# One tile more for split weights, one raw slot less, and expert weights through all slots in one turn

## Chip, core and metric

The kernel runs on one core of a Trainium2 chip. The metric is the device time of one execution in microseconds (us), and smaller is better. Engines: TensorE (PE in the rows; PEld is its weight load), VectorE (DVE), ScalarE (ACT), GpSimd (POOL) and SyncE (SP), whose queue issues nearly all transfers from device memory.

## What is computed

256 tokens of width 2048 in float32 go through a first block of two layers and a second block of one layer with experts. Cut to what matters:

```python
def first_block(x, ...):
    for l in range(2):
        proj = rms_norm(x, norm_g[l]) @ w_in[l]          # 2048 x 6726
        # three attentions on slices of proj: decay heads, latent heads (w_uq, w_ukv),
        # and differential heads; each gated with silu
        x = x + concat([a_out, b_out, c_out]) @ w_out[l]  # 2048 x 2048
    return rms_norm(x, final_norm_g)

def second_block(x, c, ...):
    mod = silu(c) @ w_ada + b_ada                         # six rows of 2048
    proj = modulate(rms_norm(x, g_mix), ...) @ w_in       # two banded attentions
    x = x + gt1 * (concat([norm(o_a), norm(o_b)]) @ w_out)
    h = modulate(rms_norm(x, g_ffn), ...)
    for e in range(32):                                   # top 1 group, top 2 experts in it
        a = silu(h @ w_gate[e]) * (h @ w_up[e])           # 2048 x 512 each
        y = y + combine[:, e:e+1] * (a @ w_down[e])       # 512 x 2048
    x = x + gt2 * y
    modf = silu(c) @ w_ada_final + b_ada_final
    return modulate(rms_norm(x, g_final), ...)
```

## The kernel before

**Projections.** Weights stream through on-chip memory once. `wload` (line 131) takes a "raw" slot (`rawt`, line 116; four slots of 1 MB, 8 KB on each of 128 partitions) and issues a load of up to four blocks of 128 rows by 512 columns on SP's queue. `proj` (line 301) goes over the four raw tiles of a projection; each raw tile is split in two halves. `wsplit` (line 269) takes an "hl" tile, also 1 MB (three slots), and `split` (lines 265 to 267) fills it from half a raw tile: ScalarE casts the weights to the high part (L266) and VectorE subtracts it from them for the low part (L267). `mm` then does three matmul passes (high by high, high by low, low by high), with the weights as the stationary operand (L291) or the moving one (L295): 24 matmuls of 256 columns or 12 of 512 for an hl tile of 512 columns. `uq` and `qsplit` split in their own order of columns, into hl tiles too.

**Modulation on the side.** After each hl tile `tick` advances a generator (`ada_gen`, line 546) at a rate of 0.59: it loads a 0.5 MB piece of `w_ada` into one of three "araw" slots on SP's queue (L543) and lets VectorE multiply it by a column of silu(c) and add it (L561), two pieces ahead.

**Experts.** Each of the 32 experts has eight 1 MB tiles for gate and up (`load_gu`, line 1174) and four for down (`load_d`, line 1193). The slots are those of the projections and no others: `etile` (line 1154) hands out the next of a list of tags, here nine (five "xm" of the seven slots of the transposed activations, one hl, the "ada" accumulator, two hl) to gate and up tiles; down tiles take the four raw slots. The first expert's loads begin while the last output projection runs (line 1204), three of them in slots of another tag ("p", `ewp` in the rows). Four experts are gathered at a time (`quad`); after the first four, two xm tiles are taken for the accumulator y. Down weights of the last expert come as strips (`load_d_strip`, line 1201).

**Order.** The lists of the engines are not written out by hand. The tile framework walks the program, gives out slots when they come free in its own estimate of time, and so fixes the order on each engine and queue; on the chip each queue keeps that order. A load into a slot waits on its queue for the slot's last user.

Of the kernel before, what the change touches and what calls it, by code (L numbers as in the profile page):

```python
# [10 lines left out]
F32 = mybir.dt.float32  # L11
F32R = mybir.dt.float32r
# [8 lines left out]
P = 128  # L21
D = 2048
# [72 lines left out]
def tile_kernel(tc, a, out, dbg=None):  # L95
# [8 lines left out]
    big = es.enter_context(tc.tile_pool(name="big", bufs=1))  # L104
# [9 lines left out]
            nc.sync.dma_start(dbg[name], ap)  # L114

    def rawt(shape, name):
        return big.tile(shape, F32, tag="raw", bufs=4, name=name)

    def pslot(shape, dt, name):
        return big.tile(shape, dt, tag="p", bufs=7, name=name)  # L120

    def small(n, name):
        return sm.tile([P, n], F32, tag=f"s{n}", name=name)
# [3 lines left out]
    def uid(s):  # L127
        cnt[0] += 1
        return f"{s}{cnt[0]}"

    def wload(w, k0, nk, n0, n, name):
        t = rawt([P, nk, n], name)
        nc.sync.dma_start(t, w[k0 * P : (k0 + nk) * P, n0 : n0 + n].rearrange("(k p) n -> p k n", p=P))
        return t
# [130 lines left out]
    def split(dst_hi, dst_lo, src):  # L265
        A.copy(dst_hi, src)  # L266
        V.tensor_sub(dst_lo, src, dst_hi)  # L267

    def wsplit(view, name, n):
        t = big.tile([P, 2, 2, 512], F32R, tag="hl", bufs=3, name=name)  # L270
        split(t[:, 0, :, :n], t[:, 1, :, :n], view)
        return t

# [2 lines left out]
    def tb_ops(n, bank=0):  # L276

        return [("T", P * i, P, bank + i // 2, 256 * (i % 2)) for i in range(n)]

    def nb_ops(c, m):  # L280

        return [("N", c, m, tb, 0, tb) for tb in range(2)]

    def mm(acc, started, w, xk, ops, last):
        for op in ops:
            kind, c, m, b, o = op[:5]
            for j, (u, v) in enumerate(PASS):
                st = b not in started
                started.add(b)
                if kind == "T":  # L290
                    T.matmul(acc[:m, b, o : o + 256], w[:, u, c : c + m], xk[v], start=st, stop=last and j == 2,  # L291
                             skip_group_check=True)
                else:
                    tb = op[5]
                    T.matmul(acc[:, b, o : o + m], xk[v][:, P * tb : P * tb + P], w[:, u, c : c + m], start=st,  # L295
                             stop=last and j == 2, skip_group_check=True)

    def accum(name=None):
        return pa.tile([P, 2, 512], F32, tag="acc", name=name or uid("acc"))

    def proj(w, n0, n, xT, ops, qs=(0, 1, 2, 3), acc=None, started=None, final=True, k0=0, splitter=None, pre=None, mid=None, by_op=False):

        acc = accum() if acc is None else acc
        started = set() if started is None else started
        for q in qs:
            raw = wload(w, k0 + 4 * q, 4, n0, n, uid("raw"))
            raws = [raw[:, 2 * hf : 2 * hf + 2, :] for hf in range(2)]
            if pre:
                pre(q)
            end = final and q == qs[-1]  # L310
            hls = []
            for hf in range(2):
                hl = (splitter or wsplit)(raws[hf], uid("hl"), n)
                hls.append(hl)
                if end and by_op:
                    continue
                for kk in range(2):
                    mm(acc, started, hl[:, :, kk, :], [xT[q][:, v, 2 * hf + kk, :] for v in range(2)], ops,
                       end and hf == 1 and kk == 1)
                if mid and hf == 0:  # L320
                    mid(q)
                tick()
            if end and by_op:
                for op in ops:
                    for k in range(4):
                        mm(acc, started, hls[k // 2][:, :, k % 2, :], [xT[q][:, v, k, :] for v in range(2)], [op], k == 3)
        return acc
# [32 lines left out]
    def xTtile(name):  # L360
        return big.tile([P, 2, 4, S], F32R, tag="xm", bufs=7, name=name)
# [237 lines left out]
    def layer(l, xT, ssq):  # L599
# [65 lines left out]
        def rope(dst, src):  # L665
            ps = pt.tile([P, 512], F32, tag="tp", name=uid("rp"))
            T.matmul(ps[:, :S], cst["perm"], src, start=True, stop=True)
            t = wk.tile([P, S], F32, tag="m", bufs=3, name=uid("rt"))
            V.tensor_mul(t, ps[:, :S], cst["sinT"])
            V.tensor_mul(dst, src, cst["cosT"])  # L670
            V.tensor_add(dst, dst, t)
# [11 lines left out]
        def uq():  # L683
            qn = pslot([P, 6, S], F32, uid("qn"))
            for u in range(3):
                acc = accum()
                started = set()
                for hf in range(2):
                    hl = big.tile([P, 2, 2, 512], F32R, tag="hl", bufs=3, name=uid("hl"))
                    raw = wload(a["w_uq"][l], 2 * hf, 2, 384 * u, 384, uid("raw"))  # L690
                    v4 = raw.rearrange("p k (h c) -> p k h c", h=2)
                    for c0, c1, o in ((0, 128, 0), (128, 192, 256)):
                        w_ = c1 - c0
                        for kk in range(2):
                            dh = hl[:, 0, kk, o : o + 2 * w_].rearrange("p (h c) -> p h c", h=2)
                            dl = hl[:, 1, kk, o : o + 2 * w_].rearrange("p (h c) -> p h c", h=2)
                            split(dh, dl, v4[:, kk, :, c0:c1])
                    for kk in range(2):
                        mm(acc, started, hl[:, :, kk, :], [c_[:, 2 * hf + kk, :] for c_ in cqT], tb_ops(3),
                           hf == 1 and kk == 1)  # L700
                A.copy(qn[:, 2 * u : 2 * u + 2, :], acc[:, 0, :].rearrange("p (j t) -> p j t", j=2))
                qr = wk.tile([P, S], F32, tag="m", bufs=3, name=uid("qr"))
                A.copy(qr, acc[:, 1, 0:S])
                rope(ropes[:, u, :], qr)
            return qn
# [40 lines left out]
        if l == 0:  # L746
            startup_rest()
            ada_start()
        rope(ropes[:, 3, :], kr[:, 0, :])
        qn = uq()  # L750
        kn, vb = ukv()
        if l == 0:
# [4 lines left out]
        for h in range(6):  # L757
# [5 lines left out]
            t = wk.tile([P, 384], F32, tag="t", bufs=3, name=uid("t"))  # L763
# [43 lines left out]
        for h in range(6):  # L807
# [4 lines left out]
            t = wk.tile([P, 384], F32, tag="t", bufs=3, name=uid("t"))  # L812
# [15 lines left out]
        for g in range(2):  # L828
            t = pslot([P, 4, S], F32, uid("cqk"))
# [26 lines left out]
        for h in range(4):  # L856
            ts_, rs = [], []
            halves = [slice(64 * i, 64 * i + 64) for i in range(2)]
            for ps in scores_pair([[(qsl(cqh[z, h, :]), ckh[z, h, :])] for z in halves]):
                t = wk.tile([P, 384], F32, tag="t", bufs=3, name=uid("t"))  # L860
# [77 lines left out]
    with tc.high_priority():  # L938
        vs = []
        for ss in (ssq, ssq1):  # L940
            t = small(2, uid("rr_s"))
# [3 lines left out]
        t = small(2, "rr_t")  # L945
# [8 lines left out]
    for q in range(4):  # L954
        t = xTtile(uid("hT"))
# [19 lines left out]
    w_in = a["w_in_2"][0]  # L975

    def qsplit(view, name, n):
        t = big.tile([P, 2, 2, 512], F32R, tag="hl", bufs=3, name=name)
        for hf in range(2):
            src = view[:, :, 256 * hf : 256 * hf + 256].rearrange("p k (r c) -> p k r c", c=64)  # L980
            dh, dl = [t[:, v].rearrange("p k (r a c) -> p k r a c", a=2, c=64)[:, :, :, hf, :] for v in range(2)]
            split(dh, dl, src)
        return t
# [157 lines left out]
    def add_half(s, acc, r):  # L1141
        for tb in range(2):
            xs = x[:, tb, 512 * s : 512 * s + 512]
            u = wk.tile([P, 512], F32, tag="stage", bufs=3, name=uid("u"))
            V.scalar_tensor_tensor(u, acc[:, tb, :], r[:, tb : tb + 1], gt1(s), op0=OP.mult, op1=OP.mult)
            V.tensor_add(xs, xs, u)

    for s in range(4):
        add_half(s, proj(a["w_out_2"][0], 512 * s, 512, mT2b, nb_ops(0, 512), qs=(0, 1), k0=8), rb_)
    wtags = ["xm"] * 5 + ["hl", "ada", "hl", "hl"]  # L1150
    wbufs = {"raw": 4, "hl": 3, "xm": 7, "ada": 1}
    wn = [0]

    def etile(shape, tag=None):
# [5 lines left out]
    def eload(src, shape, tag=None):  # L1160
        t = etile(shape, tag)
        nc.sync.dma_start(t, src)
        return t
# [25 lines left out]
    def d_rows(e):  # L1189

        return a["w_down_2"][0, e].rearrange("(p j) n -> p j n", j=4)

    def load_d(e):
        r = {}
        for f in range(4):
            t = eload(d_rows(e)[:, f, :], [P, D], "raw")
            for s in range(4):
                r[f, s] = t[:, 512 * s : 512 * s + 512]
        return r

    def load_d_strip(e, c0, n, f, nf):
        return eload(d_rows(e)[:, f : f + nf, c0 : c0 + n], [P, nf, n], "raw")

    gu0 = load_gu(0, GU0[:6])

# [224 lines left out]

    gu0.update(load_gu(0, GU0[6:]))
    d0 = load_d(0)

    def rows(c, t):
# [53 lines left out]
    for q in range(LAST + 1):  # L1488
        i = q % 2
        for b in range(NQ):  # L1490
            e = NQ * q + b
# [33 lines left out]
    for c0, n in STRIPS:  # L1525
        m = n // 4
        nf = 2048 // n
# [59 lines left out]
```

## Time and profile before

| What | us |
|---|---|
| median of three runs (2361.89, 2363.03, 2366.7) | 2363.03 |
| the profiled execution's own time | 2382.56 |
| its span, first to last instruction | 2380.9 |
| TensorE busy (89% of the span) | 2118.8 |
| TensorE weight load busy (64%) | 1512.5 |
| VectorE busy (53%) | 1252.7 |
| ScalarE busy (33%) | 793.1 |

The mean granted clock of TensorE is 0.949 of full speed, and 760.82 MB move at a mean of 320 GB/s. The busy time of TensorE is modelled (its matmuls are pipelined), so the waits say more than the shares. Rows of waits give the engine and line that waited, what it waited for, the time in total, how often, and the longest. Rows of a timeline give start and length, engine, line, operation, output and inputs, a count, and in brackets the idle time before it with what ended it. "SPq" is an issue on SP's queue.

### The profile page before, as it was taken

How to read it: one execution, taken by the hardware profiler on the slowest of the kernel's cores; microseconds unless marked ns; L12 is line 12 of the kernel's file. 1: busy time of each engine (PE TensorE's matmuls, PEld its weight loads, DVE VectorE, ACT ScalarE, POOL GpSimd, SP SyncE). 2: the span in 40 equal slices, each digit the busy share in tenths (PEclk: the TensorE clock that was granted, in tenths of full speed). 3: DMA queues.
4: the chain of work that ended last, by engine and by line, in shares of the span. 5: the costliest groups of instructions: out<-in, count | busy, mean ns of one | idle time of the engine just before them, and what ended most of it. 6: DMA issues, size and time to landing. Idle time of an engine off the chain costs nothing. (4 is left out here: it accounts for less than half of the span.)

```text
span 2380.9 us, 32560 instructions
## 1 busy us (share of the span) xinstructions
PE 2118.8 (89%) x12919; PEld 1512.5 (64%) x12919; DVE 1252.7 (53%) x1990; ACT 793.1 (33%) x1583; POOL 99.9 (4%) x149
## 2 busy tenths in 40 slices
PE   8999999999999999899999988869677878686975
PEld 8989997789899977798786774324232424241421
DVE  5786687876776877776766871202121212121323
ACT  5453645545535545545555421101010101010111
POOL 0000100000100000202001000000000000000000
PEclk9999999999999999999999989989898989899998
DMA  6688796786787876796856889999999999999995
GB/s 216 217 300 289 229 332 242 244 297 190 249 312 248 306 272 219 226 341 187 319 195 222 297 325 376 421 421 422 421 420 421 421 421 421 421 420 421 421 421 239
DMA packets 220888, 760.82 MB, mean 320 GB/s; under 512 B 22448, under 2 KB 43260, under 8 KB 172344
## 3 DMA queue, kind: packets, MB, share of 16 engines
q1 hardware_dynamic: 215576, 750.88, 83.3%
q0 software_dynamic: 4960, 7.71, 1.4%
q8 instruction: 103, 1.69, 0.3%
q14 instruction: 57, 0.47, 0.1%
q10 hardware_dynamic: 192, 0.08, 0.0%
HBM read 755.68 MB, written 2.97 MB: 319 GB/s over the span
## 5 line engine op out<-in xcount | busy, mean ns | idle before, releaser
L266 ACT CAST hl<-raw 128x1024 fp32r<-128x1024 f32 (+4 forms) x478 | 423.8, 897 | 503.0 <-PE acc L291 252.5
L267 DVE TENSOR_TENSOR hl<-raw,hl 128x1024 fp32r<-128x1024 f32 (+4 forms) x478 | 487.7, 1033 | 145.9 <-ACT hl L266 145.0
L291 PE MATMUL acc<-xT,hl 128*128 128x256 f32 x3744 | 471.7, 286 | 8.6 <-DVE hl L267 5.6
L291 PEld LDWEIGHTS acc<-xT,hl 128*128 128x128 f32 x3744 | 458.1, 193 | 14.3 <-DVE hl L267 6.7
L561 DVE SCALAR_TENSOR_TENSOR ada<-araw,cact,ada 128x1024 f32<-128x1024 f32 x240 | 307.2, 1287 | 96.2 <-DMA araw<-in_w_ada_dram 79.9
L1393 PE MATMUL gu<-ew,xe 128*32 128x512 f32 x1528 | 237.7, 634 | 89.3 <-DMA ew<-in_w_up_dram 59.4
L1406 DVE SCALAR_TENSOR_TENSOR eth<-eth,guT 128x128 f32<-128x128 f32 x32 | 9.2, 288 | 448.6 <-ACT eth L1405 448.6
L1398 ACT COPY gus<-gu 128x512 f32<-128x512 f32 x32 | 18.8, 586 | 615.5 <-PE gu L1393 615.5
L1393 PEld LDWEIGHTS gu<-ew,xe 128*32 128x32 f32 x1528 | 51.7, 113 | 261.7 <-issue 103.4
L295 PE MATMUL acc<-hl,mT 128*128 128x512 f32 x768 | 188.4, 397 | 1.7 <-DVE hl L267 1.7
L1415 PE MATMUL acc<-ew,aT 128*32 128x512 f32 x992 | 159.1, 772 | 23.9 <-DVE aT L1408 22.2
L291 PE MATMUL acc<-hT,hl 128*128 128x256 f32 x1248 | 168.7, 289 | 2.9 <-DVE hl L267 2.9
L291 PEld LDWEIGHTS acc<-hT,hl 128*128 128x128 f32 x1248 | 156.2, 193 | 12.6 <-issue 9.2
L295 PEld LDWEIGHTS acc<-hl,mT 128*128 128x128 f32 x768 | 141.9, 189 | 34.4 <-issue 3.7
L295 PE MATMUL acc<-hl,xT 128*128 128x512 f32 (+1 forms) x768 | 158.1, 367 | 5.4 <-DVE hl L267 5.4
L295 PEld LDWEIGHTS acc<-hl,xT 128*128 128x128 f32 x768 | 132.3, 190 | 30.4 <-DVE hl L267 7.8
L1371 PEld LDWEIGHTS xg<-oh,xres 128*128 128x128 f32 x512 | 122.8, 328 | 36.8 <-issue 26.8
L1419 DVE TENSOR_TENSOR y<-acc,gt2A 32x512 f32<-32x512 f32 x93 | 63.6, 684 | 148.1 <-PE acc L1415 147.1
L1371 PE MATMUL xg<-oh,xres 128*128 128x128 f32 x512 | 131.4, 411 | 5.4 <-ACT C L1362 3.2
L1393 PE MATMUL gu<-ew,xet 128*32 128x512 f32 x504 | 93.4, 663 | 35.3 <-DMA ew<-in_w_up_dram 26.0
L295 PE MATMUL acc<-hl,oT 128*128 128x512 f32 x384 | 101.6, 413 | 0.2 <-DVE hl L267 0.2
L1415 PEld LDWEIGHTS acc<-ew,aT 128*32 128x32 f32 x992 | 32.8, 133 | 103.7 <-issue 62.6
(339 smaller groups left out, 2017.5 us busy)
## 6 DMA issues: line engine op xcount, KB each, us to landing
ew<-in_w_up_dram SPq DMA_DIRECT2D x128, 1024.0 KB, 19.8
ew<-in_w_down_dram SPq DMA_DIRECT2D x128, 1024.0 KB, 19.8
ew<-in_w_gate_dram SPq DMA_DIRECT2D x126, 1024.0 KB, 19.8
raw<-in_w_in_dram SPq DMA_DIRECT2D x124, 1024.0 KB, 7.1
araw<-in_w_ada_dram SPq DMA_DIRECT2D x192, 512.0 KB, 6.3
raw<-in_w_out_dram SPq DMA_DIRECT2D x48, 1024.0 KB, 6.4
araw<-in_w_ada_final_dram SPq DMA_DIRECT2D x64, 512.0 KB, 6.3
raw<-in_w_in_dram SPq DMA_DIRECT2D x16, 512.0 KB, 3.6
```

The costliest lines, as they stand in the source:

```text
L266: A.copy(dst_hi, src)
L267: V.tensor_sub(dst_lo, src, dst_hi)
L291: T.matmul(acc[:m, b, o : o + 256], w[:, u, c : c + m], xk[v], start=st, stop=last and j == 2, skip_group_check=True)
L295: T.matmul(acc[:, b, o : o + m], xk[v][:, P * tb : P * tb + P], w[:, u, c : c + m], start=st, stop=last and j == 2, skip_group_check=True)
L561: V.scalar_tensor_tensor(ah, raw, ck, ah, op0=OP.mult, op1=OP.add)
L1371: T.matmul(ps[:, m * j : m * j + m], quads(x[:, tb, :], k), oh[:, tb, :], start=j + tb == 0, stop=tb == 1, skip_group_check=True)
L1393: T.matmul(ps[c : c + CAP, :], xe(i, k + d)[:, CAP * b : CAP * b + CAP], gu(v, k + d), start=k == 0, stop=k == KT - 2, skip_group_check=True)
L1398: A.copy(g, ps)
L1406: V.scalar_tensor_tensor(th, th, 1.0, v4[:, :, 0:CAP], op0=OP.add, op1=OP.mult)
L1415: T.matmul(acc[CAP * s : CAP * s + CAP, 0, :], aT[:, f, :], wd(f, s), start=f == 0, stop=f == 3, skip_group_check=True)
L1419: V.tensor_mul(yv(i, s)[CAP * b : CAP * b + CAP, :], acc[h, 0, :], gt2(s)[h, :])
```

## The change

Raw slots go from four to three and hl slots from three to four, so the memory is the same. The list of tags for expert tiles gets 13 entries in place of nine, all slots of all four tags (xm five), and down tiles and the last expert's strips take the next of this list instead of a raw slot. The whole diff but for the third and fourth place where an hl tile is taken (`uq`, `qsplit`), which change in the same way:

```diff
     def rawt(shape, name):
-        return big.tile(shape, F32, tag="raw", bufs=4, name=name)
+        return big.tile(shape, F32, tag="raw", bufs=3, name=name)
...
     def wsplit(view, name, n):
-        t = big.tile([P, 2, 2, 512], F32R, tag="hl", bufs=3, name=name)
+        t = big.tile([P, 2, 2, 512], F32R, tag="hl", bufs=4, name=name)
         split(t[:, 0, :, :n], t[:, 1, :, :n], view)
         return t
...
-    wtags = ["xm"] * 5 + ["hl", "ada", "hl", "hl"]
-    wbufs = {"raw": 4, "hl": 3, "xm": 7, "ada": 1}
+    wtags = ["xm"] * 5 + ["hl", "raw", "raw", "raw", "hl", "ada", "hl", "hl"]
+    wbufs = {"raw": 3, "hl": 4, "xm": 7, "ada": 1}
...
     def load_d(e):
         r = {}
         for f in range(4):
-            t = eload(d_rows(e)[:, f, :], [P, D], "raw")
+            t = eload(d_rows(e)[:, f, :], [P, D])
             for s in range(4):
                 r[f, s] = t[:, 512 * s : 512 * s + 512]
         return r
 
     def load_d_strip(e, c0, n, f, nf):
-        return eload(d_rows(e)[:, f : f + nf, c0 : c0 + n], [P, nf, n], "raw")
+        return eload(d_rows(e)[:, f : f + nf, c0 : c0 + n], [P, nf, n])
```

## Rows read from the trace of the kernel before

**Rows 1.** Busy time by windows: length, engines, clock, share of DMA engines, GB/s
```profile
0.00:1400.00 1400.00, 1350.13 (x8787) 1186.60 (x8787) 1031.40 (x1492) 702.44 (x1336) 94.73 (x142) 0.99 0.76 259
...
1500.00:2300.00 800.00, 634.45 (x3373) 259.38 (x3369) 164.53 (x342) 67.87 (x182) 0.54 (x1) 0.90 1.01 421
```

**Rows 2.** Waits over the whole span
```profile
ACT hl L266 <- PE acc L291: 252.5, 162, 3.4
...
PE acc L295 <- DVE hl L267: 11.3, 9, 4.0
...
PE acc L291 <- DVE hl L267: 8.5, 6, 3.4
```

**Rows 3.** Timeline of TensorE, four places where it waited for a split
```profile
55.83 27.67 PE L291 MATMUL acc<-xT,hl 128*128 128x256 f32 x226 [0.92 <-DVE hl L267]
...
525.93 7.03 PE L291 MATMUL acc<-xT,hl 128*128 128x256 f32 x34 [3.36 <-DVE hl L267]
...
856.63 3.54 PE L295 MATMUL acc<-hl,xT 128*128 128x512 f32 x8 [2.61 <-DVE hl L267]
...
1137.46 7.88 PE L295 MATMUL acc<-hl,hT 128*128 128x512 f32 x22 [3.98 <-DVE hl L267]
```

**Rows 4.** Timeline of VectorE ahead of the last of these waits
```profile
1134.99 1.28 DVE L561 SCALAR_TENSOR_TENSOR ada<-araw,cact,ada 128x1024 f32<-128x1024 f32 x1 [5.47 <-DMA araw<-in_w_ada_final_dram]
1136.19 2.35 DVE L267 TENSOR_TENSOR hl<-raw,hl 128x1024 fp32r<-128x1024 f32 x2
```

**Rows 5.** Windows of 20 us, columns as in rows 1
```profile
520.00:540.00 20.00, 16.64 (x118) 16.44 (x117) 11.39 (x15) 8.57 (x21) 0.69 (x1) 0.83 0.71 242
...
1120.00:1140.00 20.00, 14.97 (x106) 13.85 (x105) 9.26 (x8) 6.21 (x7) 5.87 (x12) 0.91 1.05 326
```

**Rows 6.** Timeline of SP's queue: issues in two stretches of projections
```profile
834.62 0.38 SPq L133 DMA_DIRECT2D raw<-in_w_in_dram  x1
...
849.26 6.54 SPq L543 DMA_DIRECT2D araw<-in_w_ada_dram  x2
...
1116.93 0.41 SPq L133 DMA_DIRECT2D raw<-in_w_in_dram  x1
```

**Rows 7.** Timeline of ScalarE in the same stretches
```profile
849.33 1.05 ACT L266 CAST hl<-raw 128x1024 fp32r<-128x1024 f32 x1
...
853.61 1.05 ACT L266 CAST hl<-raw 128x1024 fp32r<-128x1024 f32 x1 [1.67 <-PE acc L295]
...
1117.35 1.05 ACT L266 CAST hl<-raw 128x1024 fp32r<-128x1024 f32 x1 [1.83 <-PE acc L291]
1120.23 1.05 ACT L266 CAST hl<-raw 128x1024 fp32r<-128x1024 f32 x1 [1.83 <-PE acc L291]
...
1130.17 1.05 ACT L266 CAST hl<-raw 128x1024 fp32r<-128x1024 f32 x1 [3.13 <-PE acc L291]
```

**Rows 8.** Raw tiles: landing, 800 to 880 us; issues and landing, 1100 to 1150
```profile
DMA to landing us min/median/max: 7.2/7.6/8.3
...
L133 SPq DMA_DIRECT2D raw<-in_w_in_dram x6: 368/382/407, 1102.1 to 1147.0; - x6
...
DMA to landing us min/median/max: 6.4/12.7/17.7
```

**Rows 9.** Page, DMA issues: count, size, median time to landing
```profile
raw<-in_w_in_dram SPq DMA_DIRECT2D x124, 1024.0 KB, 7.1
```

**Rows 10.** Waits of SP's queue, first 400 us
```profile
SPq L133 <- DVE hl L267: 178.1, 52, 6.3
```

**Rows 11.** Timeline of SP's queue at the start of the experts
```profile
1438.24 0.33 SPq L1183 DMA_DIRECT2D ew<-in_w_up_dram  x1
1445.54 2.90 SPq L1162 DMA_DIRECT2D ew<-in_w_down_dram  x4
```

**Rows 12.** Timeline of TensorE: the first expert's last gate and up matmuls
```profile
1439.71 1.02 PE L1393 MATMUL gu<-ew,xe 128*32 128x512 f32 x2
```

**Rows 13.** Window of 5 us at the same place, columns as in rows 1
```profile
1440.00:1445.00 5.00, 5.00 (x34) 2.75 (x36) 0.58 (x2) 0.83 (x2) 0.00 (x0) 1.00 0.43 180
```

More of the change, by code (lines that the diff above doesn't have):

```diff
@@ L688, in uq @@
                 for hf in range(2):
-                    hl = big.tile([P, 2, 2, 512], F32R, tag="hl", bufs=3, name=uid("hl"))
+                    hl = big.tile([P, 2, 2, 512], F32R, tag="hl", bufs=4, name=uid("hl"))
                     raw = wload(a["w_uq"][l], 2 * hf, 2, 384 * u, 384, uid("raw"))
@@ L977, in qsplit @@
     def qsplit(view, name, n):
-        t = big.tile([P, 2, 2, 512], F32R, tag="hl", bufs=3, name=name)
+        t = big.tile([P, 2, 2, 512], F32R, tag="hl", bufs=4, name=name)
         for hf in range(2):
```

## The prediction

> **What bounds the kernel now.** I read the windows first. They show two regimes [rows 1]. For the first 1400 us TensorE is busy 1350 us of 1400 at a granted clock of 0.99 while the transfers run at 259 GB/s: the projections and attention are bound by TensorE. From 1500 to 2300 us the share of the DMA engines is 1.01 at 421 GB/s and TensorE is busy 79%: the 32 experts are bound by their weights' arrival, 1 MB (1.0486e6 bytes) in 2.49 us. So a gain in the first regime reaches the end only by letting the experts' stream start earlier, and in the second regime nothing but a hole in the stream can be closed.
>
> Then the waits [rows 2]. ScalarE's cast, the first half of a split, stands 252.5 us in 162 waits for matmuls of one kind of projection alone: that is a wait for a free "hl" tile, and no row of the waits has it waiting for the landing of a raw tile. So raw slots are ample and hl slots are what the splits queue for. TensorE in turn loses 11.3 + 8.5 = 19.8 us in 15 waits for the second half of a split. The timeline of TensorE has the single waits [rows 3]: 3.98 and 3.36 us, then 2.61, the other twelve shorter. What stands behind the longest is in VectorE's timeline [rows 4]: it sits 5.47 us at an "ada" instruction whose raw row has not landed, and the split that TensorE needs is queued behind it. The two-slot lead of hl (one tile in use, two ahead) is too short for such a hitch.
>
> **The change, part by part.**
>
> *Fourth hl tile.* The number and shape of casts and subtractions stay; a split may start one tile earlier. A tile lasts TensorE 2.88 us (casts at 1117.35 and 1120.23, paced by it [rows 7]); where the extra latent projection uses 18 instead of 24 matmuls per tile, 2.16. Each wait shrinks by that: 3.98 to 1.10, 3.36 to 1.20, and 2.61 and all shorter ones to nothing. I leave the 0.92 us at 55.83 us, where the first layer's inputs are still arriving. Gain 19.8 - 1.10 - 1.20 - 0.92 = 16.6 us; bounds 0 (the order on VectorE puts the ada instruction ahead of the split of every tile TensorE still has) and 19.8. I take 16.6, because the subtraction takes 1.2 us [rows 4] and the cast 1.05 [rows 7], so that a tile more in hand is a real 2.88 us. Next late is TensorE itself.
>
> *Clock.* The 20 us around two of these waits had a granted clock of 0.83 and 0.91, a loss of 3.4 + 1.8 = 5.2 us [rows 3, 5]. The waits that remain there are a third as long, but both windows hold other small work too. Bounds 0 and 5.2; I take half, 2.6 us.
>
> *Three raw slots.* A raw load is issued when the second half of an older raw tile has been split. With four slots its own first cast is the seventh after the issue, with three the fifth. From the load at 834.62 that is 853.61 against 849.33, so a lead of 19.0 us becomes 14.7; the load at 1116.93 keeps 13.2 us [rows 6, 7]. Landing takes 7.2 to 8.3 us in the first stretch and 6.4 to 17.7, median 12.7, in the second, where the code also loads the bias bands of the attention heads [rows 8]. So landing is hidden in the plain stretches by half its size, and in 1100 to 1150 us the slowest load would come 17.7 - 13.2 = 4.5 us late. The four hl tiles leave TensorE 3 x 2.88 - 1.05 - 1.2 = 6.4 us of cover for that. Bounds 0 and 27 us (all six loads of that stretch [rows 8] 4.5 late and no cover); I take one such load, 4.5 us.
>
> *SP's queue.* SP issues raw and ada loads in one order, so a raw load that waits for its slot holds the ada loads behind it, and the reverse. SP already waits 178.1 us of the first 400 for splits, in 52 waits [rows 10]: it always runs up to the slot limit. With three slots it reaches the limit one raw earlier, and the splits free slots half a raw earlier; the pace of one slot per 5.76 us is the same. Cost 0; the other bound is priced in rival 2. The Trainium skill ("DMA: Bandwidth & Descriptors", section on the anatomy of one DMA) speaks against a shorter ring: the wait for a semaphore sits on the issuing sequencer, before dispatch, so everything behind it waits too. The trace agrees in that SP's waits are listed at its own queue. By that rule alone the time would be that of the second rival, 2374 us, and by the row of SP's unchanged pace it is no cost.
>
> *Experts' tiles in one turn of 13.* Before, nine slots for gate and up and four for down; after, 13 in one turn, as many bytes and as many loads. In the steady stretch nothing can come of it: the engines are full, and cost and gain are 0 while that cover lasts. A hole is open only at the start. The stream runs at 180 GB/s from 1440 to 1445 us [rows 13], because the next load, expert 1's first down tile, waits for its slot from 1438.24 to 1445.54 [rows 11], until expert 0's down product has used the old one. After, that tile takes an hl slot whose last user is expert 0's gate/up matmul ending at 1440.73 [rows 12]. One megabyte moves into the hole: 2.5 us gained; bounds 0 and 2.5 x 3 = 7.5. The last expert's strips keep their place behind its gate and up weights in a full queue: 0.
>
> **Sum**: 16.6 + 2.6 + 2.5 - 4.5 = 17.2 us. Against the profiled execution's 2382.56 us (span 2380.9) that is 2365.4; the median of the runs is 19.5 us under the profiled one, and I carry the difference over: 2363.03 - 17.2 = 2345.8, so 2346 us.
>
> **Rivals.**
> 1. *The waits move.* The list order on VectorE and SP shifts with the slots, ada's late rows still stand before the needed split, and TensorE waits about as long elsewhere. For it: the cause in [rows 4] is a late ada row, which an hl tile does not hasten. Against: 13 of 15 waits are shorter than one tile. Left is the hole at 1440: 2363.0 - 2.5 = 2360.5 us.
> 2. *Slower: raw loads become the bound.* A raw slot's turn is landing, plus SP's delay, plus 5.2 us until its second half is split (2.88 + 1.05 + 1.2). SP was once held 6.54 us at two ada loads [rows 6]. In a plain stretch (7.6 + 6.5 + 5.2) / 3 = 6.4 us per raw against TensorE's 5.76: 0.7 lost per load so held; with four slots 4.8, nothing. In the crowded stretch (12.7 + 6.5 + 5.2) / 3 = 8.1: 2.4 lost, six times, 14 us. If a quarter of the 124 large loads of the input weights [rows 9] are so held, 31 x 0.7 = 22. Together 36 - 21.7 of gains = 14, less what the fourth hl tile covers in the crowded stretch (some 3): 2374 us. It decides from about 15 held loads on (10 + 11 = the gains). Against it: without such a hold the turn is 4.3 us.
> 3. *The one turn breaks the experts' stream.* Two of the seven "xm" slots become the accumulator after the first four experts, and down tiles now need xm too. One tile's gap for each of the eight groups of four would cost 8 x 2.5 = 20 us and take all the rest back: 2366 us. Against: 421 GB/s over 800 us without a dip [rows 1].
>
> **How the numbers follow.** Forecast case 0.55 (2334 to 2354: waits all gone and the clock whole, no late raw, 19.8 + 5.2 + 2.5 = 27.5 under the median; or half the wait gain, 8.3 + 2.5 = 10.8 under, less a little). Rival 1 0.23, rival 2 0.16, rival 3 0.06. About 0.2%, 4.7 us, is what a measurement tells from no change. Faster (under 2358.3): 0.55 + 0.08 of rival 1, which may keep a few of the waits' microseconds = 0.63. Same: 0.15 of rival 1, 0.04 of rival 2, 0.04 of rival 3 = 0.23. Slower (over 2367.7): 0.12 + 0.02 = 0.14. The range 2334 to 2368 leaves out rival 2's upper part and a little below.
>
> **What the profile after would show.** Right: TensorE's waits for splits under 8 us in all, the longest about 1.2; the windows at the two places back near clock 1.00; expert 1's first down tile issued right after expert 0's last gate/up matmul, some 5 us before its other three; 421 GB/s afterwards as before; the experts' stream full some 17 us earlier. Wrong: rows with ScalarE's cast waiting for a raw tile's landing, or longer waits by VectorE for ada rows (rival 2); a dip below 421 between 1500 and 2300 us (rival 3); 15 waits of the same sum at other places (rival 1). What would make it wrong most easily is a new order of VectorE's and SP's lists, which no row of this trace shows.

## The result and the profile after

The changed kernel takes 2381.57 us (median of 5 runs, 2379.13 to 2389.51), the kernel before beside it 2366.7 us (5 runs). The ratio is 1.0068, interval 1.005 to 1.0086: slower, where 2346 us and faster were forecast. Its profiled execution has a span of 2377.5 us (2379.13 us as timed).

The two regimes are as they were [rows 1]. Windows of the kernel after, columns as there:

```profile
0.00:1400.00 1400.00, 1351.09 (x8787) 1188.78 (x8787) 1032.29 (x1493) 701.43 (x1336) 96.90 (x142) 0.98 0.77 260
1500.00:2300.00 800.00, 626.46 (x3368) 256.41 (x3364) 161.02 (x335) 67.38 (x181) 0.54 (x1) 0.92 1.01 421
```

The stream of expert weights still fills the DMA engines at 421 GB/s, so the loss has to lie before it. TensorE stands idle 48.9 us of the first 1400, where it stood 49.9 before: its idle time did not shrink. Waits of the kernel after in its first 1400 us (engine, line, what it waited for: us in total, times, longest):

```profile
ACT hl L266 <- DMA raw<-in_w_in_dram: 43.2, 18, 6.2
...
ACT hl L266 <- DMA raw<-in_w_out_dram: 19.5, 4, 5.8
...
PE pT L449 <- ACT t L444: 5.8, 2, 5.6
...
PE rbT L258 <- DMA rbs<-in_rel_bias_b_dram: 4.9, 1, 4.9
...
PE acc L291 <- DVE hl L267: 3.7, 3, 1.9
...
PE s L420 <- DVE t L1039: 2.8, 2, 2.6
...
PE acc L295 <- DVE hl L267: 2.5, 4, 1.3
```

TensorE's waits for a split did shrink, from 19.8 us in 15 [rows 2] to 3.7 + 2.5 = 6.2 us in 7. But ScalarE's casts now wait 62.7 us for raw tiles to land, which no row of before showed, and TensorE waits elsewhere: for "rbs" (a 16 KB table of position biases), for which it did not wait before, and longer for the softmax (L444 5.8 us against 3.3, L1039 2.8 against 0.2).

At the start of the experts the forecast order is there. SP's timeline in the kernel after:

```profile
1436.56 0.33 SPq L1183 DMA_DIRECT2D ew<-in_w_up_dram  x1
1438.28 7.63 SPq L1162 DMA_DIRECT2D ew<-in_w_down_dram  x4
```

And the window that answers to [rows 13]:

```profile
1440.00:1445.00 5.00, 5.00 (x45) 2.24 (x48) 0.57 (x2) 0.28 (x1) 0.00 (x0) 1.00 0.85 292
```

The first of four down tiles is issued at 1438.28, where it stood until 1445.54 [rows 11], and the hole is half filled: 292 GB/s for 180.

One thing about the yardstick. The profiled execution of before (2382.56 us) is the slowest seen of that kernel: 28 runs of it on one other chip lay between 2360.22 and 2373.43 us. Its waits for splits were large too. The kernel e4 below has the same slots in the projections and a profiled execution of 2367.53 us, close to its median of 2366.12; from here on it stands for "four raw, three split tiles". A stage of one execution shows what was late in it; how far executions of one layout lie apart is in the table under e13 to e16.

### The profile page after: what moved, and what is told of

It reads as the page before. It is cut to its first block, busy times and chain, and to the rows that moved or that the text cites. A ratio compares the mean times of both kernels' runs of the same rounds, so it can differ in the third digit from the quotient of the medians.

```text
span 2377.5 us, 32611 instructions
## 1 busy us (share of the span) xinstructions
PE 2111.9 (89%) x12919; PEld 1513.4 (64%) x12919; DVE 1253.5 (53%) x1990; ACT 792.1 (33%) x1583; POOL 102.1 (4%) x149
## 4 chain that ended last, share of the span: by engine, by line
PE 50%; DMA 29%; issue 11%; DVE 6%; ACT 2%; POOL 0%; SPq 0%; DVEq 0%; ACTq 0%; POOLq 0%
PE acc L291 20%; DMA ew<-in_w_up_dram 15%; PE acc L295 13%; DMA ew<-in_w_down_dram 6%; DMA araw<-in_w_ada_dram 4%; PE xg L1371 3%; PE gu L1393 2%; DVE ada L561 2%; PE acc L1415 2%; DVE hl L267 2%; PE s L420 2%; DMA araw<-in_w_ada_final_dram 1%; DMA raw<-in_w_in_dram 1%; PE pT L449 1%; PE guT L1401 1%
## 5 line engine op out<-in xcount | busy, mean ns | idle before, releaser
L1371 PEld LDWEIGHTS xg<-oh,xres 128*128 128x128 f32 x512 | 122.8, 328 | 35.8 <-issue 25.9
L1371 PE MATMUL xg<-oh,xres 128*128 128x128 f32 x512 | 131.3, 409 | 5.4 <-ACT C L1362 3.2
L1393 PE MATMUL gu<-ew,xet 128*32 128x512 f32 x504 | 87.4, 619 | 34.2 <-DMA ew<-in_w_up_dram 26.3
## 6 DMA issues: line engine op xcount, KB each, us to landing
ew<-in_w_up_dram SPq DMA_DIRECT2D x128, 1024.0 KB, 19.8
ew<-in_w_down_dram SPq DMA_DIRECT2D x128, 1024.0 KB, 19.8
ew<-in_w_gate_dram SPq DMA_DIRECT2D x126, 1024.0 KB, 19.8
```

The lines of the kernel that those rows point to most:

```text
L1371: T.matmul(ps[:, m * j : m * j + m], quads(x[:, tb, :], k), oh[:, tb, :], start=j + tb == 0, stop=tb == 1, skip_group_check=True)
L1393: T.matmul(ps[c : c + CAP, :], xe(i, k + d)[:, CAP * b : CAP * b + CAP], gu(v, k + d), start=k == 0, stop=k == KT - 2, skip_group_check=True)
```

## The experiments

Theory at the outset: the slot counts carry the loss, through late raw loads. Rival: the one turn over all slots breaks the order of the experts' loads. Unless told otherwise, ratios are to the kernel before on the same chip.

**e1, e2: both kernels again.**

> The kernel before, unchanged, to see a profile beside runs of the same chip. The profile read for the prediction took 2382.56 us, its other runs 2361.9 to 2370. If that execution was untypical, the span now is 2360 to 2368 us, and the place where some 15 us are missing can be read against the old profile. If a profile always costs this kernel some 16 us, the span is again near 2381.

> The kernel after, unchanged, on the same chip as the others: 2379 to 2386 us, ratio 1.005 to 1.009 again.

e1: 2365.41 us, 0.9991 (0.9977 to 1.0005). e2: 2383.51 us, 1.0065 (1.0049 to 1.0081). The loss is 15 to 18 us on another chip too. e1 did not settle its question: its profiled execution took 2378.95 us (span 2377.3), above its other eleven, and has 18.0 us of waits for splits in 13. So both profiled executions of before lie above its usual time. e4's, below, does not, so a profile does not always do this, and what lengthens the two stays open.

**e3: the counts alone; e4: the turn alone.**

```
e3:  raw bufs=3, hl bufs=4; gate and up: xm*5, hl, ada, hl, hl; down: raw, raw, raw, hl
e4:  raw bufs=4, hl bufs=3; wtags = xm*5, hl, raw*4, ada, hl, hl
```

> Three raw and four hl slots, but gate and up tiles keep their list of nine and down tiles take three raw slots and one hl slot. Theory A (raw tiles land too late with three slots): all of the loss, ratio 1.005 to 1.009, about 2381 us. Theory B (the one turn of 13 slots disturbs the experts' stream): no loss, 0.993 to 1.000.

> Four raw and three hl slots as before, with all expert tiles in one turn of 13. Theory A: no loss, 0.998 to 1.001, the hole at the start of the experts' stream shorter by about 2.5 us. Theory B: the whole loss, 1.005 to 1.009.

e3: 2380.02 us, 1.0053 (1.0037 to 1.0069). e4: 2366.12 us, 0.9988 (0.9974 to 1.0001). The counts carry the loss; the turn costs nothing, and its forecast 2.5 us are too small to be told from nothing either.

Where the loss lies shows when the span is cut at the same matmuls in both kernels. The first matmul of the experts (L1371) starts at 1406.4 us in e4 and 1418.9 in e2, so 12.5 of the 15.1 us between the spans are lost before it. Two stages of ten carry most: from the first matmul of the modulation (adaLN, L567) to layer 0's output projection, and the second mixer's projections. The windows of e4 (columns as in [rows 1]):

```profile
270.60:341.50 70.90, 70.74 (x553) 65.67 (x553) 62.72 (x88) 37.74 (x75) 6.36 (x10) 1.00 0.95 326
...
981.10:1192.80 211.70, 203.07 (x1372) 176.93 (x1370) 161.06 (x218) 114.43 (x223) 33.38 (x55) 0.98 0.80 274
```

The same stages of e2:

```profile
273.80:351.00 77.20, 72.87 (x552) 66.35 (x552) 61.38 (x87) 38.19 (x75) 8.98 (x14) 0.96 0.94 307
...
985.20:1203.50 218.30, 209.15 (x1392) 182.44 (x1390) 162.44 (x220) 115.28 (x224) 32.70 (x55) 0.96 0.80 273
```

They are 6.3 and 6.6 us longer, with a lower clock in both. In the first, TensorE stands at L258. Its timeline in e4:

```profile
286.26 0.32 PE L258 MATMUL rbT<-ident,rbs 16*128 16x16 f32 x3
...
288.30 2.21 PE L223 MATMUL ps_relb<-oh,rbTs 128*16 128x384 f32 x6
```

In e2:

```profile
292.41 0.42 PE L258 MATMUL rbT<-ident,rbs 16*128 16x16 f32 x3 [4.33 <-DMA rbs<-in_rel_bias_b_dram]
...
294.98 3.83 PE L223 MATMUL ps_relb<-oh,rbTs 128*16 128x384 f32 x6
```

TensorE waits 4.33 us for a table of 16 KB, and the six matmuls behind it take 3.83 us instead of 2.21, at a lower granted clock. In the second stage the raw tiles are late themselves. ScalarE in e2:

```profile
1138.98 1.06 ACT L266 CAST hl<-raw 128x1024 fp32r<-128x1024 f32 x1 [3.17 <-DMA raw<-in_w_in_dram]
...
1146.95 2.18 ACT L266 CAST hl<-raw 128x512 fp32r<-128x512 f32 x4 [5.34 <-DMA raw<-in_w_in_dram]
1154.25 0.62 ACT L266 CAST hl<-raw 128x512 fp32r<-128x512 f32 x1 [5.11 <-DMA raw<-in_w_in_dram]
...
1159.15 2.18 ACT L266 CAST hl<-raw 128x512 fp32r<-128x512 f32 x4 [1.81 <-DMA raw<-in_w_in_dram]
```

In e4 no cast of this stretch waits for a raw tile; they wait for matmuls, that is for a free split tile. The raw tiles did not land more slowly in e2: from 1100 to 1150 us landing took 7.4 to 12.9 us, median 8.3, against 6.5 to 17.6, median 11.1, in e4. They were issued too late. SP's timeline in e2:

```profile
1130.00 0.38 SPq L133 DMA_DIRECT2D raw<-in_w_in_dram  x1
1132.41 7.02 SPq L543 DMA_DIRECT2D araw<-in_w_ada_final_dram  x3
1139.49 0.43 SPq L133 DMA_DIRECT2D raw<-in_w_in_dram  x1
1142.57 3.85 SPq L543 DMA_DIRECT2D araw<-in_w_ada_final_dram  x3
1146.52 0.39 SPq L133 DMA_DIRECT2D raw<-in_w_in_dram  x1
```

These are the loads of the first three casts shown. ScalarE stood ready for them 5.8, 2.1 and 2.6 us after the issue. The load at 1130.00 waited for its raw slot. The other two went out directly behind adaLN loads, and SP's waits between 1130.4 and 1146.6 us are all for those, none for a raw slot. In e4 a raw load stands behind 9.44 us of adaLN issues too (issued at 1136.74), and with four slots no cast waits for it.

In e2 the late splits bunch up on VectorE ahead of the softmax's first step (L1039, at 1162.21 us against 1157.39 in e4), and TensorE waits for that. TensorE's timeline in e2:

```profile
1162.91 2.08 PE L420 MATMUL s<-kb,qb 64*128 64x128 f32 x8 [3.39 <-DVE t L1039]
```

And in e4:

```profile
1158.90 0.93 PE L420 MATMUL s<-kb,qb 64*128 64x128 f32 x8
```

Up to these matmuls the stage is even: 177.7 us from its start in e2, 177.8 in e4, where TensorE had stood 3.89 and 1.52 us for splits. The 6.6 us are lost behind the wait, where the rest of the stage takes 40.6 us against 33.9: the granted clock is 0.50 in e2 from 1162.9 to 1170 us, and 1.00 in e4 from 1158.9 to 1165.

The next three experiments ask what these two places are worth and what makes them.

**e5: rbs from another queue.** The load is issued from POOL's queue.

```
-        nc.sync.dma_start(rbs, a["rel_bias_b_2"][0])
+        nc.gpsimd.dma_start(rbs, a["rel_bias_b_2"][0])
```

> The changed kernel with one small load, rbs, issued from POOL's queue instead of SP's. Theory A (SP's queue, longer in hand with three raw slots, brings rbs late, and the stall and the half clock behind it cost 6 to 7 us of the 12.5 lost before the experts): PE's wait of 4.3 to 4.9 us near 292 us shrinks below 1 us, the stage from the first adaLN matmul to the second layer-0 norm loses 5 to 7 us, 2376 to 2378 us, ratio 1.003 to 1.004. Rival B (the load is only the last of several late things there, so another takes its place): the stage keeps its length, 2383 us, ratio 1.0065.

2389.37 us, 1.0093 (1.007 to 1.0117): 5.9 us above e2 by the medians, though the intervals overlap. POOL's timeline of e5 around the load:

```profile
288.07 0.30 POOL L239 MEMSET bias<- 64x256 f32 x1 [4.65 <-DMA bias<-dr_t]
288.94 0.52 POOL L252 DMA_DIRECT2D rbs<-in_rel_bias_b_dram  x1 [0.56 <-DVE mn L433]
```

POOL is in order too. The load stood behind a memset that itself waited 4.65 us, was issued at 288.94 instead of 283.20 us, and TensorE's wait grew to 7.18 us. The experiment did not free the load, it delayed it. It cannot tell whether an earlier rbs would help.

**e6: the raw slot alone.** Three raw slots, three split tiles, one turn of 12.

```
raw bufs=3, hl bufs=3; wtags = xm*5, hl, raw*3, ada, hl, hl
```

> Three raw slots with three split tiles, the experts in one turn of 12: the raw count alone. Theory A (the missing raw slot makes both new waits): the wait for rbs is 4 us or more, the wait for the softmax behind late splits near 1163 us 2 us or more, and the waits for a split tile are back as well: 2384 to 2390 us, ratio 1.007 to 1.010. Rival B (the fourth split tile makes them, by putting other work ahead on PE and more transfers into the same stretch): neither wait is there, 2366 to 2369 us, ratio 0.999 to 1.001.

2386.93 us, 1.0081 (1.0063 to 1.01). The raw slot alone costs as much as the whole change, or more: 20.8 us between the medians of e6 and e4 (the kernel before took 2367.5 and 2367.6 us on their chips). Its waits in the first 1400 us:

```profile
ACT hl L266 <- DMA raw<-in_w_in_dram: 30.4, 12, 6.7
...
PE acc L291 <- DVE hl L267: 9.1, 8, 2.3
...
PE acc L295 <- DVE hl L267: 8.6, 8, 3.4
```

Casts wait for raw tiles, and splits come late as with three split tiles. But the wait for rbs is not there (its stage takes 71.4 us), and the one of L420 for L1039 is 1.85 us. So neither theory was right as a whole: the late raw tiles come with having only three raw slots, the wait for rbs with the fourth split tile.

**e7, e8: transfers taken out of the second mixer.** In both, 62 of the 64 loads of the final adaLN weights are left out; VectorE's work on them stays. e7 has the slots of after, e8 those of e4.

```
-                    raw = big.tile([P, 1024], F32, tag="araw", ...)
-                    nc.sync.dma_start(raw, ...)
+                    if v < 6 or k + h == 0:
+                        raw = big.tile([P, 1024], F32, tag="araw", ...)
+                        nc.sync.dma_start(raw, ...)
```

> The changed kernel with 62 of the 64 loads of the final adaLN weights left out (32 MB; VectorE's work on them is kept and reads one tile over and over, so the final modulation is not the reference's). Theory A (in the stage from 981 to 1193 us the transfers are what comes late, because three slots give the queue too little in hand where 16 DMA engines are nearly full): the stage is within 2 us of the same stage of e8, PE's wait for the softmax is under 1 us, and the whole gap to e8 shrinks from 17.4 to 9 to 12 us. Rival B (the order of VectorE's and PE's work with four split tiles makes it, whatever the loads do): the stage stays 5 to 7 us longer than in e8 and the gap stays at 16 to 19 us.

> Four raw slots and three split tiles in one turn, with the same 62 loads left out: the other side of the comparison with e7. Both theories: faster than e4 by up to 8 us, 2357 to 2366 us, ratio 0.995 to 0.999, since PE waits 8.6 us in that stage with all loads and not all of it is for transfers.

e7: 2365.15 us, 0.9985 (0.9973 to 0.9997). e8: 2354.2 us, 0.9939 (0.9923 to 0.9956). The gap falls from 17.4 us (e2 to e4) to 11.0; e8 itself gained 12 us on e4, more than the 8 expected. The stage in e7's windows:

```profile
992.20:1199.20 207.00, 203.36 (x1368) 177.85 (x1366) 165.29 (x223) 113.85 (x221) 32.15 (x55) 0.98 0.65 214
```

And in e8's:

```profile
983.60:1191.00 207.40, 203.60 (x1382) 178.30 (x1380) 164.55 (x222) 115.33 (x224) 31.39 (x55) 0.99 0.64 212
```

The same length, where e2 and e4 differ by 6.6 us. Without the adaLN loads three slots are nearly enough: casts wait 8.4 us for raw tiles in e7's stage, 40.3 in e2's. So in this stage the loss hangs on these transfers. The edit takes them off the DMA engines (share 0.64 instead of 0.80) and off SP's queue at once, so it does not say which of the two makes the raw tiles late. From about 1109 us on VectorE's list is in a slightly different order as well, so that the order plays no part is not shown. What is left of the gap lies in the stage of the rbs table: 79.7 us in e7, 70.9 in e8.

**e9: rbs loaded 170 us early**, into a tile of its own.

```
 def startup_rest():
+    rbs = cp.tile([48, 129], F32, name="rbs")
+    nc.sync.dma_start(rbs[0:16, 0:P], a["rel_bias_b_2"][0][:, 0:P])
+    nc.sync.dma_start(rbs[32:48, :], a["rel_bias_b_2"][0][:, P:257])
```

> The changed kernel with rbs loaded some 170 us early, in startup_rest, into a tile of its own (two loads of 16 rows), so that neither a queue nor a shared staging buffer can make it late. Theory A (PE's wait of 4.3 to 7.2 us for rbs and the half clock behind it are 7 us of the loss): no wait for rbs, the stage from the first adaLN matmul to the second layer-0 norm back to 71 to 73 us from 77 to 80, 2374 to 2378 us, ratio 1.003 to 1.0045. Rival B (PE comes there too early because splits are late, so the next late thing, a split or the oh table, takes the wait over): stage 76 us or more, 2381 to 2385 us.

2384.02 us, 1.0053 (1.0037 to 1.0069), not to be told from e2 and e3. The wait for rbs is gone, and another stands at its place. TensorE's timeline in e9:

```profile
293.05 1.09 PE L449 MATMUL pT<-ident,t 128*128 128x128 f32 x3 [3.78 <-ACT t L444]
```

ScalarE's:

```profile
291.65 1.04 ACT L266 CAST hl<-raw 128x1024 fp32r<-128x1024 f32 x1 [4.32 <-DMA raw<-in_w_in_dram]
292.60 0.80 ACT L444 ACTIVATE t<-t,r 128x128 f32<-128x128 f32 x2
```

Rival B holds. On ScalarE a cast whose raw tile lands 4.32 us late stands ahead of the softmax's scaling (L444), which needs no weights at all. In e2 the first users of the rbs table and of that raw tile start within 0.2 us of each other (292.41 and 292.28 us): the small table was the last name on a stretch in which everything was late. The theory that the rbs load is worth 7 us by itself has fallen.

**e10 to e12: four and four, with other buffers cut.** There is no room for it as the kernel stands, so all three have AHEAD 1 (two araw slots) and two stage and two t buffers.

```
AHEAD = 1; stage bufs=2; t bufs=2;   e10: raw 4, hl 4    e11: raw 4, hl 3    e12: raw 3, hl 4
```

> Four raw slots and four split tiles, the experts in one turn of 14. To make room three other buffers are cut (AHEAD 1, so two araw slots; two stage and two t buffers), in e11 and e12 too, so these three are compared with each other. Theory A (the fourth split tile is worth what PE waits for splits in a 4-and-3 run with normal timing, 13 us, less the 6 that stay with four: 6 to 10 us with its clock): 6 to 10 us faster than e11. Rival B (the 16.6 us of the forecast were right and only the raw slot ate them): 14 to 18 us faster than e11. Rival C (a fourth split tile is worth nothing, since late work only moves): within 3 us of e11.

> The same three cuts with four raw slots and three split tiles in one turn. Slower than e4 by what the cuts cost, an estimate of 5 to 30 us, by both theories.

> The same three cuts with three raw slots and four split tiles in one turn. Theory A (a raw slot is worth 15 to 22 us, as e6 against e4 showed, and a split tile 6 to 10): 15 to 22 us slower than e10 and 7 to 15 slower than e11. Rival B (with fewer araw transfers in hand the stream of the adaLN weights no longer fills the DMA engines, so the raw slot costs less): within 5 us of e10.

e10: 2398.27 us, 1.0118 (1.0099 to 1.0137). e11: 2419.29 us, 1.02 (1.0179 to 1.022). e12: 2429.43 us, 1.025 (1.0231 to 1.0269). Here the split tile is worth 21 us, more than any of e10's expectations, and the raw slot 31, more than e12's. The cuts cost e11 53 us, more than estimated, so this is another kernel: VectorE waits 122.9 us for adaLN rows in e11's first 1400 us, 65.4 in e4's, and TensorE 16.8 + 13.7 = 30.5 us for splits (e10: 8.4 + 6.3). Where VectorE's hitches are that long, a split tile more is worth what the forecast gave it, and more.

**e13 to e16: four and four, with one xm tile less.** This leaves the adaLN prefetch whole.

```
xm bufs=6;   e13: raw 4, hl 4    e14: raw 4, hl 3    e15: raw 5, hl 3    e16: raw 3, hl 4
```

> Four raw slots and four split tiles, room made by one xm tile less (six for seven: the tiles of the normed strips and of the mixers' outputs); everything else as in the kernel before, adaLN prefetch too. Theory A (the fourth split tile is worth more where a fourth raw slot feeds it: 21 us in e10 against e11, 3 in e2 against e6): 12 to 20 us faster than e14. Rival B (it is worth 3 to 8 us, and e10's 21 came from the shorter adaLN prefetch): 3 to 8 us faster than e14.

> Four raw slots, three split tiles, six xm tiles: what the xm tile is worth by itself. An estimate of 0 to 15 us slower than e4 by either theory.

> Five raw slots, three split tiles, six xm tiles. Theory A (a raw slot is worth some 20 us from three to four, since a missing MB is late where the DMA engines are full, and less from four to five): 3 to 10 us faster than e14. Rival B (four slots already cover every late load, as the ten PE waits of the kernel before for splits and none for raw loads say): within 3 us of e14.

> Three raw slots, four split tiles, six xm tiles. Theory A (the raw slot's price at four split tiles is the 31 us of e12 against e10 less what the cuts added): 18 to 31 us slower than e13. Rival B (it is the 17 us of the whole change): under 14 us slower than e13.

e13: 2441.98 us, 1.0315 (1.0295 to 1.0334). e14: 2436.77, 1.0284 (1.0259 to 1.0308). e15: 2437.11, 1.0293 (1.0269 to 1.0317). e16: 2448.53, 1.0322 (1.0299 to 1.0344). By the whole time e13's and e14's expectations fell: e13 is not faster than e14, and the xm tile cost 70 us instead of 0 to 15. e15 is within 3 us of e14 and e16 6.6 us slower than e13, as their rivals said, but the xm tile's 70 us weigh on that. Those lie in the experts, whose stream no longer holds 421 GB/s. e14:

```profile
1500.00:2300.00 800.00, 610.51 (x3096) 243.83 (x3099) 149.30 (x318) 59.58 (x165) 0.54 (x1) 0.89 0.94 387
```

Before the experts the tile costs nothing: their first matmul starts at 1406.3 us in e14 and at 1406.4 in e4. So the counts can be compared there. "rbs stage" and "second mixer" are the two stages of above, the first from the first adaLN matmul to the first one of the output projection, the second from the first matmul of L961 to that of L1013. e17 and e18, below, have the slots of e13. Each kernel stands for one execution:

| raw slots, split tiles | kernels | rbs stage, us | second mixer, us | start of the experts, us |
|---|---|---|---|---|
| 4, 3 | before, e1, e4, e14 | 69.7 to 70.9 | 211.9 to 213.6 | 1417.0, 1412.7, 1406.4, 1406.3 |
| 5, 3 | e15 | 69.7 | 213.8 | 1406.1 |
| 4, 4 | e13, e17, e18 | 74.2 to 76.6 | 212.3 to 216.0 | 1403.5, 1414.9, 1411.2 |
| 3, 3 | e6 | 71.3 | 217.1 | 1423.4 |
| 3, 4 | after, e2, e3, e16 | 77.2 to 79.6 | 217.3 to 219.1 | 1415.4, 1418.9, 1418.5, 1423.3 |

The two stages sort by the counts without overlap: the first by the split tiles (three: up to 71.3 us, four: from 74.2), the second by the raw slots (four or five: up to 216.0, three: from 217.1). So the fourth split tile costs 3 to 8 us in the rbs stage, with either number of raw slots. The starts are not so clear. before, e1 and e4 lie 10.6 us apart and e13, e17 and e18 11.4, though the instructions on ScalarE, VectorE and SP stand in the same order in the three of each up to 1300 us; e13's (2431.39 us) lies below its other five runs. On the means of the starts the raw slot costs 12.8 us with three split tiles and 9.1 with four, and the split tile brings 4.4 us with three raw slots and 0.7 with four, too little to be told from nothing. The whole time, over many executions, gives 20.8 us for the raw slot (e6 against e4) and 3.4 to 6.9 us for the split tile with three raw slots (e2 and e3 against e6, intervals that overlap). A fifth raw slot brings nothing (e15 against e14).

What became of the split tile's gain shows in e13's waits in its first 1400 us:

```profile
ACT hl L266 <- DMA raw<-in_w_in_dram: 15.4, 6, 3.8
...
PE acc L291 <- DVE hl L267: 4.9, 2, 3.1
...
PE pT L449 <- ACT t L444: 4.7, 1, 4.7
...
PE rbT L258 <- DMA rbs<-in_rel_bias_b_dram: 3.9, 1, 3.9
...
PE cum L791 <- DVE lf L789: 2.1, 1, 2.1
...
PE acc L295 <- DVE hl L267: 1.9, 1, 1.9
```

and in e4's:

```profile
PE acc L291 <- DVE hl L267: 8.3, 6, 2.6
...
PE acc L295 <- DVE hl L267: 6.5, 6, 3.9
...
PE pT L449 <- ACT t L444: 2.7, 2, 2.5
```

TensorE's waits for splits fall from 14.8 to 6.8 us, by 8.0. Those for rbs (3.9), for the softmax at L444 (4.7 - 2.7 = 2.0) and for L789 (2.1) rise by 8.0. That the two sums are equal is chance, but e17 and e18 have the same new waits (rbs 5.0 and 3.6 us, L444 4.9 and 4.7, L789 2.5 and 2.2), and all listed waits of TensorE in the first 1400 us come to 42.5 to 51.3 us in the four profiles with four and three, and to 44.6 to 49.5 in the three with four and four. With four split tiles, ScalarE's casts wait for raw tiles even with four raw slots (15.4 us of the input weights'; none in e4): the splits run one tile further ahead, up to the next limit.

**e17, e18: why one xm tile less breaks the experts' stream.** Both have e13's slots; e17 has separate lists as in before, e18 xm six times in the turn.

```
e17:  gate and up: xm*5, hl, hl, ada, hl, hl; down: raw*4
e18:  wtags = xm*6, hl, raw*4, hl, ada, hl, hl
```

> e13 (four raw slots, four split tiles, six xm tiles) with the expert weights on separate lists, as in the kernel before: gate and up tiles over xm five times, hl, hl, ada, hl, hl, down tiles over the four raw slots. Theory A (six xm tiles break the experts' stream only when all slots are in one turn): the stream is back at 421 GB/s, and the whole is e13's start of the experts, 1403.5 us, and some 959 us behind it: 2360 to 2365 us. Rival B (six xm tiles break it under either list): 2425 us or more.

> e13 with xm six times in the turn instead of five, so that the turn goes over each slot once. Theory A (five entries for six tiles let the xm tiles drift against the turn, and that breaks the stream): 421 GB/s, 2360 to 2366 us. Rival B (the room of the experts' stream is simply one tile too small or late at its start): 2420 us or more.

e17: 2422.81 us, 1.023 (1.0201 to 1.0258). e18: 2426.43 us, 1.0255 (1.0226 to 1.0284). The turn is not the cause: e18's rival holds, and e17 is 2 us under the bound of its rival and 58 above its theory. SP's timeline of e13 shows the form of it, loads in bursts with 22.8 us between two issues:

```profile
1590.66 0.33 SPq L1183 DMA_DIRECT2D ew<-in_w_up_dram  x1
1613.50 1.99 SPq L1162 DMA_DIRECT2D ew<-in_w_down_dram  x4
```

The code offers a cause: the two accumulators y (L1514) are xm tiles and stay, so of six only four are left for lists that name five or six. A list with four was not tried, so this is argued, not shown, and what four and four slots give at the end stays open. By their starts of the experts (1403.5 to 1414.9 us, where four and three have 1406.3 to 1417.0) nothing tells them from the slots of before. No version here that does the whole work beats the kernel before.

## Why the prediction was wrong

**Fourth split tile, 16.6 us: wrong size, and "next late is TensorE itself" failed.** The waits for splits went, as described. But 19.8 us was the sum of an unusually slow execution (18.0 in e1, 14.8 in e4, 12.2 in e14), and what the rest bought was spent on other waits: rbs, softmax, L789. Measured: 3.4 to 6.9 us with three raw slots, not clear of noise, and nothing that shows with four. The step sized each wait by itself and never asked what TensorE meets some microseconds later when it comes sooner. That was the first rival's mechanism, and it describes the tile's part well.

**Clock, 2.6 us: wrong sign.** The windows around the old waits did recover (1.00 and 1.00 in the kernel after), but the new ones brought their own. In e2 the windows 1145 to 1165 and 1165 to 1185 us have a granted clock of 0.92 and 0.82, in e4 1.00 and 1.00. Over the ten stages before the experts the clock that was not granted adds up to 39 us in e2 and 24 in e4 (length times what is missing to 1.00); this bounds its cost from above, since a low clock in a wait costs nothing.

**Three raw slots, 4.5 us: the step that failed most.** "I take one such load" stands against 20.8 us by the whole time (e6 against e4), within its own bound of 27. The feared landing of 17.7 us did not come; the lead of 13.2 us was wrong. In the second mixer of e2 ScalarE stood ready 5.8, 2.1 and 2.6 us after the issue, and landing took 7 to 9 us. The lead was read from a trace in which casts waited for a free split tile. With four split tiles the casts reach for a raw tile sooner, and with three raw slots the loads go out later. The estimate also let 6.4 us of split tiles cover a late load, and left out that ScalarE and VectorE run in order, so that a late cast also holds the softmax behind it (e9), and the loads of the output projections (19.5 us of the casts' waits after). "No row of the waits has it waiting for the landing of a raw tile; so raw slots are ample" was the wrong reading: the row said that four are enough, not that three are. That the late raw tiles of the second mixer come with the adaLN loads is shown by e7 and e8; for the other stages it is argued.

Against the sum, the raw slot is 16.3 us short and the split tile 9.7 to 13.2; with the 5.1 us of clock and hole, which no whole time shows, that is about the 32 us between forecast and result.

**SP's queue, cost 0: wrong in the second mixer, its size open.** Two of the late loads of e2 went out directly behind adaLN loads that SP stood at for 7.02 and 3.85 us. This is the hold that rival 2 priced with 6.54 us. The Trainium skill says in "DMA: Bandwidth & Descriptors" (anatomy of one DMA) that a wait for a semaphore is sat out on the issuing sequencer, before dispatch. Both traces agree: e2's on SP's queue, and e5's on POOL's, where rbs is issued 5.7 us later. How much of the 20.8 us the hold makes, and how much the missing slot by itself, no run separates.

**The one turn: right in its order.** No cost (e4), no dip below 421 GB/s, the hole half filled; its 2.5 us are too small to show. Rival 3 is out for these slots.

**Rival 2** had the right side and the nearest mechanism, late raw loads. Its 2374 us came from a loss per load on TensorE in the plain stretches; the runs show instead a few long waits, several of them for something other than a split, with a lower clock behind them.

## What to carry to other kernels

A ring that nobody waits on may be exactly deep enough: before taking a slot from it, look how soon after its issue each load will be wanted, in the stretch where its queue is held longest, and not on average. A stage that gets more buffers moves its wait to the next thing that is late on an in-order engine, so list what the consumer meets next before booking the gain. And compare the profiled execution with the spread of the runs before its waits go into a sum, and one layout with another only by several profiles: the starts here spread by up to 11 us, and only the single stages sorted cleanly.

## What the runs showed of the hardware

Two waits of TensorE in e2 were followed by a stretch at the lower of the clock's two levels (0.50 of full speed, 1.2 GHz). After 4.33 us at L258, the 10 us from 290 us had a granted clock of 0.66 and six matmuls took 3.83 us for 2.21; after 3.39 us at L420, the clock was 0.50 for the next 7 us and eight matmuls took 2.08 us for 0.93.

A load of 16 KB took 9.2 us in e2, from the issue to the end of TensorE's wait for it, and 5.5 us to land in e4, issued at 283.20 and 280.68 us; in both the DMA engines' share from 280 to 290 us was 1.03.
